# Encoder layer on one Trainium2 core: the softmax weights of the dilated attention tied to a later group of units

## The chip, the cores and the metric

The kernel runs on one core of one Trainium2 chip. Five engines work beside each other, each through its own instruction stream in order: TensorE (PE, matrix products, with its weight loads as PEld), VectorE (DVE), ScalarE (ACT), GpSimd (POOL) and SyncE (SP). SP computes nothing here; it issues nearly all DMA transfers. The metric is the device time of one execution in microseconds (us). Before the change the median of three runs is 2876.34 us (2875.6 to 2882.24).

## The reference

One layer of an encoder over 2048 tokens of 1024 features, in float32: a projection, two mixers side by side, an output projection, and a mixture of 16 experts. The part that matters here is the first mixer. For each of 8 heads it runs three banded attentions, with strides 1, 4 and 16 (the patterns 0, 1 and 2 of the kernel), and joins them by their softmax maxima and denominators:

```python
    m_all = jnp.stack(ms)
    scale = jnp.exp(m_all - jnp.max(m_all, axis=0, keepdims=True))
    numer = jnp.sum(scale[..., None] * jnp.stack(nums), axis=0)
    denom = jnp.sum(scale * jnp.stack(dens), axis=0)
    return (numer / denom[..., None]).reshape(B, S, ATTN_WIDTH)
```

## The kernel before

A float32 product is made of three PE products of rounded parts. The stages follow one another with overlap: projection and the recurrent mixer (to about 830 us), the 8 attention heads (about 860 to 1510 us), the rest of the output projection and the router, and the experts (from about 1730 us). Work that waits for nothing, projection columns (lines 236 to 238) in the first heads and the output projection (lines 858 to 860) in the last ones, is given the lowest priority and fills PE between the attention's products.

The order on each engine is made at build time by a scheduler: it simulates the program and takes, whenever an engine is free in that simulation, the ready instruction of the highest priority. On the chip the order is fixed: an instruction whose input has not come holds up everything behind it on its engine.

`att_head` computes one head. Its tokens are cut into 4 groups (g) of 512. A call of `four` does four units of 128 queries. For each group it does four units of pattern 0 and then four of pattern 1; the 16 units of pattern 2 stand between group 1 and group 2. A unit is: scores on PE (lines 645 and 646, into `pa`), bias and row maximum on DVE (line 657), exponential and row sum on ACT (line 658), transposes on PE (line 660, into `pb`), a copy of these to `eT` on DVE or ACT (lines 664 and 662), and the numerators on PE (line 690). Units of pattern 1 in groups 0 and 3 reach over the edge of the sequence: there POOL fills 64 columns of `ex` with zeros first (lines 648 and 650), and the transposes need them. POOL also lays out the queries (`qc`, lines 616 and 619).

The maxima and sums of the units stand in `st0` (pattern 0), `sg` (pattern 1) and `st2` (pattern 2). Those of patterns 0 and 2 go to DRAM (`st_d`, lines 759 and 783) and come back in another token order. Four steps for each group follow:

- `fetch`: two loads of `st_d` into `sg` (line 707), issued on SP
- `weights`: minimum, difference, exponential, sum, reciprocal and product (lines 716 to 722, on DVE, with line 718 on ACT), and a store to `cw_d` (line 723)
- `spread`: two loads that give every partition the weights, `wB` (line 728)
- `combine`: four elementwise steps on POOL (lines 733 to 736) that weigh and add the numerators of the patterns, `nt` and `n2`, and a store to `mixt_d` (line 738)

A list of due numbers says where each step stands in the program: the number 2g is the place behind pattern 0 of group g, 2g + 1 that behind its pattern 1, and numbers from 8 on are places in the next head. `after(k)` writes out what is due there. This sets priorities alone: nothing else keeps the scheduler from taking `weights` as soon as its input is there in the simulation. `n2` has one buffer for all heads, `cw` and `wB` have two.

Of the kernel before, what the change touches and what calls it, by code (L numbers as in the profile page):

```python
# [23 lines left out]
F32 = mybir.dt.float32  # L24
# [5 lines left out]
AF = mybir.ActivationFunctionType  # L30
OP = mybir.AluOpType
# [9 lines left out]
def dram_ap(t, off, ap):  # L41
    return bass.AP(tensor=t.tensor, offset=t.offset + off, ap=[list(a) for a in ap])
# [3 lines left out]
def encoder_layer(ctx, tc, x, norm1_w, w_in, q_norm_w, k_norm_w, lb_f, lb_b, o_norm_w, w_out,  # L46
                  norm2_w, w_router, w_gate, w_up, w_down, out):
    nc = tc.nc
    pe, act, dve, pool, sp = nc.tensor, nc.scalar, nc.vector, nc.gpsimd, nc.sync
# [482 lines left out]
    def att_load(p, T, h, g):  # L532

        u, s2 = h // 2, h % 2
        for j in range(2):

            x4 = p.tile([128, 4, 128], F32, name="x4", bufs=4)
            for c in range(2):
                sp.dma_start(x4[:, :, 64 * c:64 * c + 64],
                             dram_ap(qk_d, (u * S + g * 512) * 256 + 128 * j + 64 * s2,  # L540
                                     [[256, 128], [128 * 256, 4], [1, 64]]))
            T["x4", g, j] = x4
# [22 lines left out]
    def att_turn(T, g):  # L565

        qs = T["qs"].rearrange("p (r a) -> p r a", r=16)[:, :, 32 * g:32 * g + 32]
        kh, kl = (T[n][:, :, 16 + 128 * g:144 + 128 * g] for n in ("kh", "kl"))
        for j in range(2):
            pt = (pa, pb)[j]()  # L570
            for i in range(4):
                pe.transpose(pt[:, i * 128:(i + 1) * 128], T["x4", g, j][:, i], ident)
            if j == 0:

                pt = pt.rearrange("p (a r) -> p r a", r=16)
                act.activation(qs, pt, AF.Copy, scale=T["wq"])  # L576
                dve.scalar_tensor_tensor(qs[64:], pt[64:], T["wq"][64:], qs[64:].bitcast(F32),
                                         op0=OP.mult, op1=OP.subtract)
            else:
                pt = pt.rearrange("p (j r) -> p r j", r=4)  # L580
                act.activation(kh, pt, AF.Copy, scale=T["wk"])
                dve.scalar_tensor_tensor(kl, pt, T["wk"], kh.bitcast(F32), op0=OP.mult, op1=OP.subtract)

    def att_v2(T, h):
        sp.dma_start(T["vp"][2][:, :, :64], dram_ap(v_d, 64 * h, [[16 * 512, 128], [512, 16], [1, 64]]))

    def att_head(p, T, h):
# [79 lines left out]
        def four(pat, n4, st, out):  # L667


            per = 4 if pat == 2 else 2  # L670
            w, vp = 512 // per, vps[pat]
            pnum = pn([128, 512])[:, :256]
            qc = qs[:, n4 * 128:n4 * 128 + 512] if pat == 2 else qcs.pop((pat, n4 // 4))
            units = [unit(pat, n4 + i) for i in range(4)]
            eTs = [block(pat, qc[:, i * 128:], units[i:i + per], w, st[:, i:i + per], (n4 + i) % 8 >= 6)
                   for i in range(0, 4, per)]

            if pat == 0:
                todo = [[(hf, 2 * hf + u, slice(128 * u, 128 * u + 128)) for hf in range(2)] for u in range(2)]
            else:  # L680
                todo = [[(hf, u, slice(64 * u, 64 * u + 64)) for hf in range(2)] for u in range(4)]
            for pair in todo:
                for i in range(len(units[0][3])):
                    for hf, u, cols in pair:
                        e = eTs[u // per][:, u % per * w + i * 128:u % per * w + i * 128 + 128]
                        if pat == 1:
                            e = e[:, 64 * hf:64 * hf + 64]
                        elif pat == 2:
                            e = e.rearrange("p (g f a) -> p g f a", g=4, f=2)[:, :, hf, :]
                        pe.matmul(pnum[64 * hf:64 * hf + 64, cols], vp[:, units[u][3][i], :], e,  # L690
                                  start=i == 0, stop=i == len(units[0][3]) - 1)
            if pat == 0:
                act.activation(out, pnum, AF.Copy)
            elif pat == 1:
                act.activation(out.rearrange("p (j r) -> p j r", r=4), pnum.rearrange("p (r j) -> p j r", r=4), AF.Copy)
            else:
                act.activation(out, pnum.rearrange("p (r a) -> p a r", r=4), AF.Copy)
# [4 lines left out]
        late = T["late"]  # L702
# [6 lines left out]

        def weights(g):  # L710
            sg = grp[g][0]
            w = p.tile([128, 3, 4], F32, name="cw", bufs=2)
            m8 = p.tile([128, 4], F32, name="cm", bufs=2)
            d8 = p.tile([128, 4], F32, name="cd", bufs=2)
            wd = p.tile([128, 3, 4], F32, name="cdd", bufs=2)
            dve.tensor_reduce(m8, sg[:, :, :, 1].rearrange("p a t -> p t a"), axis=AX.X, op=OP.min)
            dve.tensor_tensor(w, m8[:, None, :].to_broadcast([128, 3, 4]), sg[:, :, :, 1], op=OP.subtract)
            act.activation(w, w, AF.Exp)
            dve.tensor_mul(wd, w, sg[:, :, :, 0])
            dve.tensor_reduce(d8, wd.rearrange("p a t -> p t a"), axis=AX.X, op=OP.add)  # L720
            dve.reciprocal(d8, d8)
            dve.tensor_mul(w, w, d8[:, None, :].to_broadcast([128, 3, 4]))  # L722
            sp.dma_start(dram_ap(cw_d, h * 3 * S + 512 * g, [[4, 128], [S, 3], [1, 4]]), w)
# [6 lines left out]

        def combine(g):
            sg, wB, nt = grp.pop(g)
            pool.tensor_mul(nt, nt, wB[:, :2])
            pool.tensor_mul(wB[:, 2], wB[:, 2], n2[:, 256 * g:256 * g + 256])
            pool.tensor_add(nt[:, 0], nt[:, 0], nt[:, 1])
            pool.tensor_add(nt[:, 0], nt[:, 0], wB[:, 2])
            for hf in range(2):
                sp.dma_start(mixt_d[g][64 * h:64 * h + 64, 256 * hf:256 * hf + 256],
                             nt[64 * hf:64 * hf + 64, 0])
# [1 line left out]
        grp = {}  # L741


        for g, ks in ((0, (4, 5, 6, 7)), (1, (4, 5, 6, 7)), (2, (5, 6, 7, 8)), (3, (7, 8, 9, 10))):
            for k, f in zip(ks, (fetch, weights, spread, combine)):
                late.append((8 * h + k, f is not combine, len(late), f, g))

        def after(k):
            for t in sorted(t for t in late if t[0] <= 8 * h + k):
                late.remove(t)  # L750
                t[3](t[4])

        for g in range(4):
            sg = p.tile([128, 3, 4, 2], F32, name="sg", bufs=4)
            nt = p.tile([128, 2, 256], F32, name="nt", bufs=4)
            grp[g] = sg, None, nt
            st0 = p.tile([128, 4, 2], F32, name="st0", bufs=2)
            four(0, 4 * g, st0, nt[:, 0])
            sp.dma_start(dram_ap(st_d, (h * S + 512 * g) * 2, [[2, 128], [256, 4], [1, 2]]), st0)
            after(2 * g)  # L760
            if g == 0:
                att_turn(T, 2)
                if h < 7:
                    att_load(p, T, h + 1, 0)
            elif g > 1 and h < 7:
                att_turn(T, g - 2)
                att_load(p, T, h + 1, g)
            if g < 3:
                qcs[0, g + 1] = queries(0, g + 1)
            four(1, 4 * g, sg[:, 1], nt[:, 1])  # L770
            if g < 3:
                qcs[1, g + 1] = queries(1, g + 1)
            after(2 * g + 1)
            if g == 0:
                att_turn(T, 3)
                if h < 7:
                    att_load(p, T, h + 1, 1)
            if g == 1:
                n2 = p.tile([128, S // 2], F32, name="n2", bufs=1)
                st2 = p.tile([128, 16, 2], F32, name="st2", bufs=1)  # L780
                for n4 in range(0, 16, 4):
                    four(2, n4, st2[:, n4:n4 + 4], n2.rearrange("p (a r) -> p a r", r=16)[:, :, n4:n4 + 4])
                sp.dma_start(dram_ap(st_d, (8 + h) * S * 2, [[32, 128], [1, 32]]), st2.rearrange("p r c -> p (r c)"))
                if h < 7:
                    att_v2(T, h + 1)
            if g and h < 7:
                att_values(T, h + 1, g - 1)
                if g == 3:
                    att_values(T, h + 1, 3)
        if h == 7:  # L790
            after(10)


    def op_setup(T):
# [128 lines left out]
    def heads(u):  # L923
        with mixer():
            for h in (2 * u, 2 * u + 1):
                att_head(ap_, AT, h)
# [384 lines left out]
```

## Time and profile before

| What | us |
|---|---|
| median of three runs | 2876.34 |
| the profiled execution, its own time | 2881.4 |
| its span, from the first to the last instruction | 2879.6 |
| PE busy with products, of the span | 2656.7 |
| DVE busy | 1772.3 |
| ACT busy | 1465.3 |
| POOL busy | 304.3 |

The trace is one execution; all positions below are us from the start of its span. PE is busy for 92% of the span and the other engines for 62% and less, so time can go where PE stands still. An idle stretch of another engine counts only where PE, sooner or later, waits for it. The page also gives the clock that PE was granted, as a share of full speed: it takes two levels, 1.0 (2.4 GHz) and 0.5 (1.2 GHz).

### The profile page before, as it was taken

The page shows a single profiled execution, that of the slowest core. Times are in us where ns is not written, and L with a number is a line of the kernel's source. Part 1 is how long each engine was busy: PE and PEld are TensorE (multiplying, and loading weights), DVE is VectorE, ACT ScalarE, POOL GpSimd, SP SyncE. Part 2 cuts the span into 40 slices and gives each one's busy share as a digit, 9 for nine tenths or more (in the row PEclk, how much of TensorE's full clock was granted, in tenths as well). Part 3 has the DMA queues.
Part 4 walks back from the last instruction along what each step waited for, and adds up shares of the span by engine and source line. Part 5 has one row for each costly group of instructions (what it writes and reads, how often), then busy time and mean ns, then how long its engine had stood idle before and what let it go on. Part 6 is the DMA issues. An engine that isn't in the chain of part 4 may idle for free.

```text
span 2879.6 us, 61971 instructions
## 1 busy us (share of the span) xinstructions
PE 2656.7 (92%) x24198; PEld 2447.7 (85%) x24198; DVE 1772.3 (62%) x4463; ACT 1465.3 (51%) x3056; POOL 304.3 (11%) x477
## 2 busy tenths in 40 slices
PE   8999999998998888978888959999999999999998
PEld 8899999998988777866665739999999999999997
DVE  6547787878855545665445675555555555555553
ACT  6536666667645545554333534444444444444442
POOL 0000000000011333333220010000000000000000
PEclk9999999999999989989998969999999999999999
DMA  8776877766677666767648625666666666666663
GB/s 297 241 247 204 242 217 243 215 211 207 205 229 166 148 139 153 145 139 163 146 104 269 230 86 182 209 209 206 205 205 206 206 207 207 207 208 209 209 199 105
DMA packets 613652, 563.31 MB, mean 196 GB/s; under 512 B 186208, under 2 KB 567136, under 8 KB 613360
## 3 DMA queue, kind: packets, MB, share of 16 engines
q1 hardware_dynamic: 603824, 525.72, 60.9%
q0 software_dynamic: 9536, 33.64, 5.2%
q8 instruction: 190, 3.11, 0.5%
q14 instruction: 102, 0.84, 0.1%
HBM read 466.50 MB, written 92.73 MB: 194 GB/s over the span
## 4 chain that ended last, share of the span: by engine, by line
PE 74%; DMA 14%; DVE 6%; SPq 2%; ACT 2%; issue 2%; POOL 1%; POOLq 0%; DVEq 0%; ACTq 0%
PE mpg L1227 9%; PE mpg L1229 9%; PE mpg L1228 9%; PE pm L238 6%; PE pm L237 6%; PE pm L236 6%; PE mpy L1262 4%; PE mpy L1264 4%; PE mpy L1263 4%; PE pn L690 2%; DMA st_d<-st 2%; PE pb L660 2%; PE pm L859 2%; PE pm L858 2%; DMA gz<-pf_d 2%
## 5 line engine op out<-in xcount | busy, mean ns | idle before, releaser
L1211 DVE TENSOR_TENSOR mlo<-mraw,mhi 128x1024 fp32r<-128x1024 f32 x384 | 470.1, 1224 | 465.7 <-ACT mhi L1210 465.2
L1210 ACT ACTIVATE mhi<-mraw 128x1024 fp32r<-128x1024 f32 x384 | 406.9, 1060 | 591.0 <-PE mpg L1228 404.2
L1227 PE MATMUL mpg<-xh,mhi 128*128 128x256 f32 x2048 | 579.6, 283 | 0.0
L1229 PE MATMUL mpg<-xh,mlo 128*128 128x256 f32 x2048 | 579.1, 283 | 0.0
L1228 PE MATMUL mpg<-xl,mhi 128*128 128x256 f32 x2048 | 576.5, 282 | 0.0
L1228 PEld LDWEIGHTS mpg<-xl,mhi 128*128 128x128 f32 x2048 | 387.5, 189 | 0.6
L1227 PEld LDWEIGHTS mpg<-xh,mhi 128*128 128x128 f32 x2048 | 386.6, 189 | 1.1 <-ACT xh L1183 0.4
L1229 PEld LDWEIGHTS mpg<-xh,mlo 128*128 128x128 f32 x2048 | 384.1, 188 | 0.0
L236 PE MATMUL pm<-whi,hth 128*128 128x256 f32 x1280 | 364.5, 286 | 16.3 <-ACT ast L178 10.4
L238 PE MATMUL pm<-whi,hlo 128*128 128x256 f32 x1280 | 369.0, 289 | 6.2 <-DMA hlo<-lo_d 6.2
L237 PE MATMUL pm<-wlo,hth 128*128 128x256 f32 x1280 | 365.7, 287 | 0.0
L236 PEld LDWEIGHTS pm<-whi,hth 128*128 128x128 f32 x1280 | 245.6, 192 | 18.9 <-ACT ast L178 10.9
L238 PEld LDWEIGHTS pm<-whi,hlo 128*128 128x128 f32 x1280 | 245.7, 192 | 8.9 <-DMA hlo<-lo_d 7.9
L237 PEld LDWEIGHTS pm<-wlo,hth 128*128 128x128 f32 x1280 | 244.8, 191 | 1.4 <-DVE wlo L171 0.4
L237 PE MATMUL pm<-hlo,whi 128*128 128x256 f32 x768 | 221.0, 288 | 2.6 <-DMA hlo<-lo_d 2.4
L236 PE MATMUL pm<-hth,whi 128*128 128x256 f32 x768 | 221.2, 288 | 2.1 <-ACT whi L170 1.1
L238 PE MATMUL pm<-hth,wlo 128*128 128x256 f32 x768 | 219.2, 286 | 3.8 <-DVE wlo L171 3.8
L1262 PE MATMUL mpy<-mhi,hh 128*128 128x512 f32 x512 | 205.9, 403 | 0.0
L1263 PE MATMUL mpy<-mlo,hh 128*128 128x512 f32 x512 | 203.9, 398 | 0.0
L1264 PE MATMUL mpy<-mhi,hl 128*128 128x512 f32 x512 | 202.9, 396 | 0.0
L690 PE MATMUL pn<-eT,vp 128*64 128x64 f32 (+1 forms) x2048 | 114.6, 246 | 53.8 <-DVE cw L722 13.4
L690 PEld LDWEIGHTS pn<-eT,vp 128*64 128x64 f32 x2048 | 87.4, 141 | 78.3 <-ACT qs L576 14.1
(349 smaller groups left out, 5512.2 us busy)
## 6 DMA issues: line engine op xcount, KB each, us to landing
hlo<-lo_d SPq DMA_DIRECT2D x480, 256.0 KB, 4.1
mraw<-in_w_expert_gate_dram SPq DMA_DIRECT2D x64, 1024.0 KB, 5.6
mraw<-in_w_expert_up_dram SPq DMA_DIRECT2D x64, 1024.0 KB, 5.0
mraw<-in_w_expert_down_dram SPq DMA_DIRECT2D x64, 1024.0 KB, 4.9
wraw<-in_w_in_dram SPq DMA_DIRECT2D x128, 128.0 KB, 3.9
x<-qk_d SPq DMA_DIRECT2D x128, 128.0 KB, 5.1
out_dram<-oxt SPq DMA_DIRECT2D x32, 512.0 KB, 5.9
pf_d<-est SPq DMA_DIRECT2D x96, 128.0 KB, 3.8
```

The costliest lines, as they stand in the source:

```text
L236: pe.matmul(o, l[0], r[0], start=kc == 0, stop=False)
L237: pe.matmul(o, l[0], r[1], start=False, stop=False)
L238: pe.matmul(o, l[1], r[0], start=False, stop=kc == KC - 1)
L690: pe.matmul(pnum[64 * hf:64 * hf + 64, cols], vp[:, units[u][3][i], :], e, start=i == 0, stop=i == len(units[0][3]) - 1)
L1210: act.activation(hi, src, AF.Copy)
L1211: dve.tensor_sub(lo, src, hi.bitcast(F32))
L1227: pe.matmul(o, hi[:, k, :], xh[:, k, :], start=k == 0, stop=False)
L1228: pe.matmul(o, hi[:, k, :], xl[:, k, :], start=False, stop=False)
L1229: pe.matmul(o, lo[:, k, :], xh[:, k, :], start=False, stop=k == KC - 1)
L1262: pe.matmul(o, hh[:, f, ts], hi[:, cs], start=f == 0, stop=False)
L1263: pe.matmul(o, hh[:, f, ts], lo[:, cs], start=False, stop=False)
L1264: pe.matmul(o, hl[:, f, ts], hi[:, cs], start=False, stop=f == KC - 1)
```

## The change

`after` now takes the statistics of the four units just written out. If something is due, ACT computes `one` from the last of their row sums: the sum times zero, plus one. `weights` begins with a product of its input `sg` with `one` on DVE (line 712 of the changed kernel), and `combine` with a product of two columns of `wB` with `one` on POOL (line 734). The values stay as they were, but both steps can now start only when the four units have ended. The due numbers of groups 2 and 3 are later, and with them the place behind the last head (11 in place of 10).

```diff
         def weights(g):
             sg = grp[g][0]
+            dve.tensor_scalar(sg, sg, T["one"], None, op0=OP.mult)
...
         def combine(g):
             sg, wB, nt = grp.pop(g)
+            pool.tensor_scalar(wB[:, ::2, 0:1], wB[:, ::2, 0:1], T["one"], None, op0=OP.mult)
...
-        for g, ks in ((0, (4, 5, 6, 7)), (1, (4, 5, 6, 7)), (2, (5, 6, 7, 8)), (3, (7, 8, 9, 10))):
+        for g, ks in ((0, (4, 5, 6, 7)), (1, (4, 5, 6, 7)), (2, (6, 7, 8, 9)), (3, (7, 9, 10, 11))):
             for k, f in zip(ks, (fetch, weights, spread, combine)):
                 late.append((8 * h + k, f is not combine, len(late), f, g))
 
-        def after(k):
-            for t in sorted(t for t in late if t[0] <= 8 * h + k):
+        def after(k, st=None):
+            due = sorted((t for t in late if t[0] <= 8 * h + k), key=lambda t: t[:3])
+            if due and st is not None:
+                T["one"] = p.tile([128, 1], F32, name="one", bufs=4)
+                act.activation(T["one"], st[:, 3, 0:1], AF.Copy, scale=0.0, bias=1.0)
+            for t in due:
                 late.remove(t)
                 t[3](t[4])
...
-            after(2 * g)
+            after(2 * g, st0)
...
-            after(2 * g + 1)
+            after(2 * g + 1, sg[:, 1])
...
-            after(10)
+            after(11)
```

The first place is on DVE in the second head (head 1, counted from 0). Before, the weights of its groups 0 and 1 stand right behind the four units of pattern 0 of group 2, whose statistics are `st0_14026`:

```order
L657 ISA ex_14046,st0_14026<-pa_14045,tab0_13564 128x256
L657 ISA st0_14026 128x1
L716 TENSOR_REDUCE cm_14156<-sg_13586 128x4
L716 TENSOR_REDUCE cm_14168<-sg_13758 128x4
L717 TENSOR_TENSOR cw_14155<-cm_14156,sg_13586 128x12
L717 TENSOR_TENSOR cw_14167<-cm_14168,sg_13758 128x12
```

Now the same weights stand behind the last units of pattern 1 of group 2 (`sg_14048`) and two units of pattern 0 of group 3 (`st0_14216`):

```order
L657 ISA ex_14143,sg_14048<-pa_14142,tab1_13583 128x256
L657 ISA sg_14048 128x1
L582 SCALAR_TENSOR_TENSOR kl_12697<-pb_14109,wk_12687,kh_12694 128x4x128
L657 ISA ex_14219,st0_14216<-pa_14218,tab0_13574 128x256
L657 ISA st0_14216 128x1
L657 ISA ex_14219,st0_14216<-pa_14218,tab0_13574 128x256
L657 ISA st0_14216 128x1
L712 TENSOR_SCALAR sg_13596<-sg_13596,one_14181 128x24
L712 TENSOR_SCALAR sg_13774<-sg_13774,one_14181 128x24
L717 TENSOR_REDUCE cm_14185<-sg_13596 128x4
L717 TENSOR_REDUCE cm_14198<-sg_13774 128x4
```

The weights moved back by six units, and each got a product with `one` in front.

The second place is on POOL, at the end of the same head. Before, the combining of group 0 and of group 1 (`nt_13587`, `nt_13759`) stood around the zeros for pattern 1 of group 3 (`ex_14293`), and ahead of a query of the next head (`qc_15628`) and the zeros for its first units of pattern 1 (`ex_15632`, `ex_15651`):

```order
L734 TENSOR_TENSOR wB_14237<-wB_14237,n2_13871 128x256
L650 MEMSET ex_14293 128x64 x2
L606 MEMSET tab0_16316 128x4x16
L616 COPY qc_15537<-qs_12693 128x128 x4
L607 MEMSET tab0_16316 128x4x16
L736 TENSOR_TENSOR nt_13587<-nt_13587,wB_14234 128x256
L735 TENSOR_TENSOR nt_13759<-nt_13759 128x256
L736 TENSOR_TENSOR nt_13759<-nt_13759,wB_14237 128x256
L619 COPY qc_15628<-qs_12693 128x512
L648 MEMSET ex_15632 128x64 x2
L648 MEMSET ex_15651 128x64 x2
```

Now (names are numbered anew: `nt_13597` and `nt_13775` are the two groups, `qc_15649`, `ex_15653` and `ex_15672` the next head's):

```order
L734 TENSOR_SCALAR wB_14264<-wB_14264,one_14348 128x2
L735 TENSOR_TENSOR nt_13597<-nt_13597,wB_14264 128x512
L736 TENSOR_TENSOR wB_14264<-wB_14264,n2_13895 128x256
L737 TENSOR_TENSOR nt_13597<-nt_13597 128x256
L734 TENSOR_SCALAR wB_14267<-wB_14267,one_14348 128x2
L738 TENSOR_TENSOR nt_13597<-nt_13597,wB_14264 128x256
L735 TENSOR_TENSOR nt_13775<-nt_13775,wB_14267 128x512
L736 TENSOR_TENSOR wB_14267<-wB_14267,n2_13895 128x256
L619 COPY qc_15649<-qs_12693 128x512
L648 MEMSET ex_15653 128x64 x2
L648 MEMSET ex_15672 128x64 x2
```

The zeros for group 3 now stand ahead of both combinings, and those of the next head still behind them.

## Rows read from the trace of the kernel before

**Rows 1.** Windows by stage: borders, length, busy per engine (count), clock, DMA share, GB/s
```profile
860.00:1510.00 650.00, 543.19 (x5068) 479.20 (x5067) 355.65 (x1347) 314.76 (x1084) 195.53 (x367) 0.92 0.65 145
1510.00:1600.00 90.00, 76.31 (x384) 55.48 (x384) 47.57 (x143) 35.41 (x73) 5.08 (x10) 0.89 0.79 262
1800.00:1872.00 72.00, 72.00 (x536) 67.28 (x535) 42.69 (x68) 34.20 (x48) 5.20 (x4) 1.00 0.65 209
```

**Rows 2.** Waits, 860 to 1600: who <- for whom: us in total, times, longest
```profile
POOL nt L733 <- DMA wB<-cw_d: 134.8, 18, 14.5
DVE cm L716 <- DMA sg<-st_d: 132.9, 23, 15.9
...
PE pn L690 <- DVE cw L722: 13.4, 2, 8.8
...
ACT n L697 <- POOL wB L734: 4.2, 2, 3.6
...
PE pb L660 <- POOL ex L650: 2.2, 1, 2.2
```

**Rows 3.** Timeline of DVE in head 1: start, length, instruction [idle before <- releaser]
```profile
981.89 0.08 DVE L657 DVE_READ_ACCUMULATOR2_ANT st<- 128x1 f32 x1
992.36 0.17 DVE L716 TENSOR_REDUCE cm<-sg 128x4 f32<-128x12 f32 x1 [10.39 <-DMA sg<-st_d]
...
1001.26 0.08 DVE L657 DVE_READ_ACCUMULATOR2_ANT st<- 128x1 f32 x1
...
1002.82 0.17 DVE L716 TENSOR_REDUCE cm<-sg 128x4 f32<-128x12 f32 x1 [1.47 <-DMA sg<-st_d]
...
1024.70 0.17 DVE L716 TENSOR_REDUCE cm<-sg 128x4 f32<-128x12 f32 x1 [9.40 <-DMA sg<-st_d]
```

**Rows 4.** Timeline of SP in the same place: stores of `st0` and `st2`
```profile
977.24 2.63 SPq L759 DMA_DIRECT2D st_d<-st x1
...
988.26 0.38 SPq L783 DMA_DIRECT2D st_d<-st x1
```

**Rows 5.** Timeline of PE in the same head
```profile
994.52 1.12 PE L690 MATMUL pn<-eT,vp 128*64 128x64 f32 x16 [7.26 <-DVE cd L720]
...
1036.28 0.87 PE L660 MATMUL pb<-ident,ex 128*128 128x128 f32 x6
```

**Rows 6.** Windows over 16 waits of line 716, to 3 us past each
```profile
982.00:995.40 13.40, 6.14 (x83) 5.75 (x81) 2.55 (x14) 4.30 (x15) 2.85 (x4) 0.88 0.49 131
...
1303.40:1312.80 9.40, 3.45 (x17) 2.70 (x16) 2.90 (x11) 2.43 (x10) 1.28 (x3) 0.83 1.03 213
...
1485.50:1499.30 13.80, 5.67 (x62) 4.30 (x62) 2.61 (x8) 1.46 (x4) 4.28 (x8) 0.81 0.30 88
sum 175.80, PE 84.76 PEld 72.64 DVE 40.43 ACT 40.34 POOL 45.27; mean PE 5.30 PEld 4.54 DVE 2.53 ACT 2.52 POOL 2.83
```

**Rows 7.** The window of head 1 among them, drawn out to 10 us past its wait
```profile
982.00:1002.40 20.40, 13.14 (x130) 11.68 (x129) 6.83 (x29) 8.53 (x29) 4.35 (x8) 0.83 0.51 108
```

**Rows 8.** Timeline of POOL at the end of head 1
```profile
1013.55 1.31 POOL L733 TENSOR_TENSOR nt<-nt,wB 128x512 f32<-128x512 f32 x1 [8.45 <-DMA wB<-cw_d]
...
1022.46 1.09 POOL L619 CAST qc<-qs 128x512 fp32r<-128x512 f32 x1
1023.49 0.41 POOL L648 MEMSET ex<- 128x64 f32 x4
```

**Rows 9.** Instructions by line: duration in ns, minimum/median/maximum
```profile
L112 ACT ACTIVATE osy<-oss x16: 192/203/203, 1558.5 to 1673.4; 128x1 f32<-128x1 f32 x16
```

**Rows 10.** The same view for line 717, beside which POOL works
```profile
L717 DVE TENSOR_TENSOR cw<-cm,sg x32: 159/170/1012, 916.7 to 1496.5; 128x12 f32<-128x12 f32 x32
```

**Rows 11.** The same view for a POOL copy of line 605
```profile
L605 POOL COPY tab<-tab x8: 288/306/476, 831.5 to 1315.2; 128x128 f32<-128x128 f32 x8
```

**Rows 12.** Timeline of DVE where line 717 took longest
```profile
1496.51 1.01 DVE L717 TENSOR_TENSOR cw<-cm,sg 128x12 f32<-128x12 f32 x1
```

**Rows 13.** Timeline of POOL at the same moment
```profile
1496.24 1.26 POOL L733 TENSOR_TENSOR nt<-nt,wB 128x512 f32<-128x512 f32 x1 [9.44 <-DMA sg<-st_d]
```

## The prediction

> **What bounds the kernel now.** I read the windows by stage first. In the experts' stage PE is busy for all of its 72 us at full clock, and the change touches nothing there [rows 1]. In the attention stage, from 860 to 1510, PE is busy for 543.2 of 650 us, so 106.8 us are idle, and the granted clock is 0.92: it stands at half for about 2 x 0.08 x 650 = 104 us [rows 1]. No other engine is near full there: DVE 55%, ACT 48%, POOL 30%.
>
> The waits say what PE stands behind. The largest on DVE is line 716, the first step of `weights`, for the statistics that come back from DRAM: 132.9 us in 23 waits, the longest 15.9. POOL waits 134.8 us for `wB`, and PE is found waiting directly for line 722, the end of `weights` [rows 2].
>
> The timelines of head 1 show one such wait. DVE ends the four units of pattern 0 of group 2 at 981.97 and then does nothing for 10.39 us until line 716 starts at 992.36 [rows 3]. PE, which needs a copy that is queued on DVE behind it, loses 7.26 us of these [rows 5]. SP shows why the data were late: the store of `st0` before it was issued at 977.24, that of `st2`, on which this fetch rests, only at 988.26, behind eleven us of other transfers in one queue [rows 4]. The scheduler's own simulation saw the data sooner and so put the weights too early.
>
> To size the loss I laid windows over the 16 longest waits of line 716, each to 3 us past its end: 175.8 us, of which PE is busy for 84.8 [rows 6]. So 91.0 of the stage's 106.8 idle us lie at these waits. Outside them PE is busy for 458.4 of 474.2 us, or 97%: without the waits nothing else in this trace holds PE for long.
>
> **The change, part by part.** *The weights move.* On DVE they now stand two to six units later. In head 1 that work takes from 992.53 to 1001.34, 8.8 us [rows 3], against a wait of 10.39: what is left, 1.6 us, is less than the 3.1 us that PE got through here (10.39 - 7.26) before it ran out [rows 3, 5]. I take the same for 14 of the 16 windows. Two are kept. Behind the last head no unit follows, so its window keeps its idle 13.8 - 5.7 = 8.1 us. In head 5 the order moves the weights by two units only, and its window (idle 9.4 - 3.45 = 6.0) keeps, I estimate, 2 [rows 6]. So 91 - 10 = **81 us** of PE's idle time go; bounds are 0 (data late by as much again) and 91.
>
> *The clock.* A long gap is followed by a stretch at half clock: the window of head 1 has 0.88, or 3.2 us at half, and drawn out by 7 us it has 0.83, or 6.9 us [rows 6, 7]; so 3.7 us of half clock fall on work after the gap, at a cost of 1.9. Over the stage's 104 us the cost lies between 0 (all idle) and 52 (all work); with half of it work it is 26. New, shorter gaps (below) will keep part of it, so I take **12**.
>
> *What is added.* 60 ACT steps on one column, 32 DVE steps on 24 columns, 32 POOL steps on two. Nearest rows: 0.203 us for an ACT step on one column [rows 9], 0.170 for a DVE step on 12 columns [rows 10], 0.306 for a POOL copy of 128 columns [rows 11], which I take as the upper end, with half of it as the lower. That makes 12.2 us on ACT, 5.4 on DVE and 4.9 to 9.8 on POOL. They lie beside PE, and the two busier engines have half the stage free; if that cover were gone, they would cost up to 27. The 32 new waits for `one` are short, since two units stand between its last sum and the weights. I take **2 us**, range 0 to 27.
>
> A DVE step can be longer beside POOL: line 717 has a median of 170 ns and a longest of 1012 [rows 10], and in that longest it ended at 1497.52, as POOL's line 733, running from 1496.24, ended at 1497.50 [rows 12, 13]. The Trainium skill (SBUF — State Buffer, Who interferes with whom) says that a DVE instruction with two SBUF inputs waits out a GpSimd instruction that reads SBUF, as the two share a port pair, and that a tensor_scalar in a two-port mode does so too; this speaks against the change, which adds such a step. The trace agrees for line 717, and no run here shows line 712. By that rule each of the 32 chains could be held once by 0.84 us, 27 us of DVE time in all, and the sum would be up to 27 us higher if PE had no cover.
>
> *What is late next.* This decides the size. On POOL the combining of groups 0 and 1 stands in both kernels ahead of one query and of the zeros that PE's transposes need in the next head's first units of pattern 1. In head 1 the chain from line 716 (992.36) over the store of the weights, `wB` and both combinings (line 733 starts at 1013.55) ends with these zeros at 1023.49 plus 0.41: 31.5 us [rows 3, 8]. It is made of two DRAM round trips in SP's queue, which the change does not shorten, and it now starts six units later. Between its new start (1001.34) and the transposes that need the zeros (1036.28) lie 34.9 us [rows 3, 5], but 1.5 and 9.4 of them are waits of line 716 that go too [rows 3]: 24.0 us. So POOL would be 7.5 us late, and with PE's cover of 3 it costs 4 to 5. Before, PE lost only 2.2 us to such zeros [rows 2], because the waits of DVE gave POOL time. There are 7 such places (each head but the last). Bounds are 0 and the 14.5 us of POOL's longest wait [rows 2], 101 in all; as other heads have more or less slack I take 3.5 each, nearer to the computed head: **25 us**.
>
> In the same way pattern 2 of the next head writes `n2`, whose one buffer the combining of group 3 still reads: ACT lost 4.2 us in two waits [rows 2]. That combining now stands two places later, but its data are asked for sooner after the weights. Range 0 to 3.6 (the longest) for each of 7 heads, nearest to 0 since PE has cover for 3: **2 us**.
>
> **The sum.** The profiled execution takes 2881.4 us: its span of 2879.6 and 1.8 around it. 2881.4 - 81 - 12 + 2 + 25 + 2 = 2817.4. The median of the runs lies 5.1 lower (2876.3), so I forecast 2812 us.
>
> **The rivals.** *No new gate:* SP has fewer transfers in the way of the store of the weights, POOL keeps pace, and the clock's part is larger: 2876.3 - 81 - 22 + 2 = 2775. For it: PE's 97% outside the waits. Against it: the 31.5 us of the chain in head 1.
>
> *The wait moves to POOL in full (slower):* each weights chain starts six units later, and PE runs into the missing zeros of every next head. It turns the result when PE's loss there passes 79 / 7 = 11.3 us a head, that is when POOL is about 14 us late in place of 7.5, as when the store of the weights and `wB` each stay 3 us longer in SP's queue. At POOL's longest wait, 14.5 us for each of 7 heads, it gives 2876.3 - 81 + 2 + 101 = 2898, and the clock is not regained.
>
> *SP sets the pace:* its queue is in order, and the store of `st2` came eleven us after the one before [rows 4]. If fetches slip as the units do, line 716 waits as before and the time stays at 2876. Against it: the transfers of the next head's rows, which fill that queue, do not grow with the move.
>
> *Half of it:* POOL's lateness takes 7.5 to 11.3 us a head in place of 3.5: 2812 - 25 + 53 to 79, or 2840 to 2866.
>
> **How the numbers follow.** A measurement of this kernel tells 0.3% from no change, 8.6 us: faster is below 2867.7, slower above 2885.0. Forecast (2790 to 2840): 0.50. No new gate (below 2790): 0.18. Half of it: 0.14. SP sets the pace, no change: 0.08. Slower by POOL: 0.10. So faster 0.50 + 0.18 + 0.14 = 0.82, same 0.08, slower 0.10. The range reaches from 2762, where even the two kept waits and all of the clock's 26 us are gone (2876.3 - 91 - 26 = 2759), to 2866, just under the cases of no change and slower, which with a tail of the first are the 2 in 10 left out.
>
> **What would show it.** The weights: line 716, now 717 and 712 on DVE, should have under 35 us of waits for `sg` in place of 132.9, most of it in the last head. PE's idle time in the stage should fall from 107 us to about 55, the stage's clock rise to 0.93 or 0.94. POOL's wait for `wB` should stay above 100 us, and PE (or its weight loads) should now wait for `ex` of line 648 or for the query of line 619, 3 to 5 us in most heads. The forecast is wrong if line 712 waits as long as line 716 did, if PE's gaps stay as many and as long under another name, or if the stages before 860 or after 1600 move.

## The result, and the profile after

| What | us |
|---|---|
| before, median of 4 runs | 2876.76 (2875.6 to 2882.24) |
| after, median of 4 runs | 2851.79 (2851.54 to 2855.2) |
| after / before | 0.9912, 95% interval 0.9895 to 0.9929 |
| the profiled execution of after: its time, its span | 2855.2, 2853.4 |

The change makes the kernel faster by 0.9%, 25 us. The forecast was 2812 us, a gain of 64. The direction was right and the time lies in the range, but more than half of the gain that I had worked out did not come. The rest of this document is about those 39 us.

The windows of after by stage, as in [rows 1] (length, then busy time and count of PE, PEld, DVE, ACT and POOL, granted clock, DMA share, GB/s):

```profile
860.00:1510.00 650.00, 555.97 (x5137) 490.24 (x5137) 372.13 (x1443) 330.81 (x1152) 209.46 (x409) 0.92 0.67 158
1510.00:1600.00 90.00, 85.09 (x509) 63.12 (x508) 52.12 (x126) 42.41 (x104) 0.00 (x0) 0.98 0.72 239
1800.00:1872.00 72.00, 72.00 (x536) 67.32 (x536) 42.13 (x67) 33.70 (x47) 5.18 (x4) 1.00 0.65 205
```

PE is idle for 650 - 556.0 = 94.0 us of the attention stage, against 106.8 before, and for 4.9 of the 90 behind it, against 13.7. That makes 21.6 us less; I had forecast some 54 (81 less 25 and 2). The stage's clock is still 0.92; behind it the clock rose from 0.89 to 0.98. The experts' stage is as it was.

Line 712, which now stands in front of the weights, in the view of one line (duration in ns, minimum/median/maximum; below it what ended the idle time before it):

```profile
L712 DVE TENSOR_SCALAR sg<-sg,one x32: 228/234/837, 916.4 to 1455.9; 128x24 f32<-128x24 f32 x32
...
its engine sat idle before it (us, times) until:
  ACT one L755: 4.7, 6
  DMA sg<-st_d: 2.2, 2
```

So the wait at which the change is aimed is gone: 2.2 us for `sg`, where line 716 had 132.9 [rows 2]. What stands in its place, from the waits of 860 to 1600 (who <- for whom: us in total, times, longest):

```profile
POOL wB L734 <- DMA wB<-cw_d: 169.2, 19, 20.7
...
ACT n L697 <- POOL wB L736: 42.0, 6, 12.2
...
ACT whi L170 <- DMA wraw<-in_w_in_dram: 25.0, 3, 14.6
...
ACT nt L693 <- DMA mixt_d<-nt: 24.9, 5, 9.9
...
PEld pb L660 <- POOL ex L648: 12.4, 5, 4.8
...
PE pb L660 <- POOL ex L648: 10.7, 4, 4.5
```

ACT waits 42.0 us to write the next head's `n2`, which the combining of group 3 still reads, against 4.2 before [rows 2]; 24.9 for an `nt` buffer whose sums have not been stored; 25.0 for the weights of the projection (`wraw`). Here is one such place, between head 0 and head 1, followed over five engines: the last product of the weights on DVE, then SP, POOL, ACT and PE (start, length, instruction [idle before <- releaser]). On DVE:

```profile
954.46 0.16 DVE L723 TENSOR_TENSOR cw<-cw,cd 128x12 f32<-128x12 f32 x1
```

On SP, where the store of these weights is line 724 and the loads of `wB` that follow from it are line 729:

```profile
956.66 1.87 SPq L554 DMA_DIRECT2D vp<-v_d  x4
...
963.12 4.51 SPq L539 DMA_DIRECT2D x<-qk_d  x4
967.73 1.14 SPq L724 DMA_DIRECT2D cw_d<-cw  x1
968.97 0.43 SPq L220 DMA_DIRECT2D hlo<-lo_d  x1
969.49 0.42 SPq L201 DMA_DIRECT2D v_d<-est  x1
969.96 2.39 SPq L539 DMA_DIRECT2D x<-qk_d  x4
972.45 1.50 SPq L766 DMA_DIRECT2D st_d<-st  x1
973.99 1.30 SPq L729 DMA_DIRECT2D wB<-cw_d  x2
```

On POOL, the combining of this group:

```profile
983.41 0.30 POOL L734 TENSOR_SCALAR wB<-wB,one 128x2 f32<-128x2 f32 x1 [8.48 <-DMA wB<-cw_d]
...
985.00 0.72 POOL L736 TENSOR_TENSOR wB<-wB,n 128x256 f32<-128x256 f32 x1
```

On ACT, the first write of the next `n2`:

```profile
985.76 0.38 ACT L697 ACTIVATE n<-pn 128x256 f32<-128x256 f32 x1 [12.18 <-POOL wB L736]
```

On PE, behind it:

```profile
986.20 1.12 PE L690 MATMUL pn<-eT,vp 128*64 128x64 f32 x16 [9.00 <-ACT n L697]
```

The weights are ready at 954.6. Their store leaves at 967.73, 13.1 us later, behind the next head's values, queries and keys (lines 554 and 539) in SP's one queue; PE pays 9.00 us at the end. The queue is not all of the delay: of the 31.6 us from the last product to PE's start, 13.1 pass before the store is issued, 6.3 from there to the load of `wB`, 9.4 until POOL has that load, and 2.8 on POOL and ACT. Measured in this way on the timelines, from the end of the last product to the issue of its store, the 32 stores of weights wait 150.4 us in all in the kernel before (median 2.9) and 196.7 in the changed one (median 6.2).

### The profile page after: what moved, and what is told of

The parts are those of the page before. It is cut to its first block, busy times and chain, and to the rows that moved or that the text cites. A ratio compares the mean times of both kernels' runs of the same rounds, so it can differ in the third digit from the quotient of the medians.

```text
span 2853.4 us, 62059 instructions
## 1 busy us (share of the span) xinstructions
PE 2647.6 (93%) x24198; PEld 2442.7 (86%) x24198; DVE 1776.7 (62%) x4495; ACT 1473.5 (52%) x3116; POOL 313.2 (11%) x509
## 4 chain that ended last, share of the span: by engine, by line
PE 73%; DMA 13%; DVE 7%; SPq 2%; ACT 2%; POOL 2%; issue 2%; POOLq 0%; DVEq 0%; ACTq 0%
PE mpg L1234 9%; PE mpg L1236 9%; PE mpg L1235 9%; PE pm L238 5%; PE pm L237 5%; PE pm L236 5%; PE mpy L1269 4%; PE mpy L1271 4%; PE mpy L1270 4%; DMA wB<-cw_d 2%; PE pn L690 2%; PE pb L660 2%; DMA gz<-pf_d 2%; PE pm L866 1%; PE pm L867 1%
## 5 line engine op out<-in xcount | busy, mean ns | idle before, releaser
L660 PE MATMUL pb<-ident,ex 128*128 128x128 f32 x640 | 117.1, 299 | 40.3 <-ACT ex L658 22.0
L238 PEld LDWEIGHTS pm<-hth,wlo 128*128 128x128 f32 x768 | 146.5, 191 | 5.2 <-DVE wlo L171 5.1
```

The lines of the kernel that those rows point to most:

```text
L238: pe.matmul(o, l[1], r[0], start=False, stop=kc == KC - 1)
L660: pe.transpose(pT[:, c:c + 128], ex[:, c:c + 128], ident)
```

## The experiments

The runs were made on several chips, so each is told as the ratio to the kernel before on the same chip, with the 95% interval. Every edit to the program makes the scheduler put part of the order anew; two edits that should cost little, b_non2 and a_sxp below, moved the time by 0.1%, which is inside their intervals, but how much another order alone can move it was not measured. On these chips the kernel before takes 2888 to 2901 us, against 2877 above, so a small difference between the windows or waits of two runs can also come from the chip. In the diffs, a line with - is the changed kernel (or the kernel before, for names with b_) and one with + the experiment.

### Are the new waits the price?

**a_non2** and **b_non2**: the combining reads `nt` in place of `n2` and so doesn't hold it. This leaves the numerators of pattern 2 out of the sum; the number and shapes of the instructions stay.

```diff
-            pool.tensor_mul(wB[:, 2], wB[:, 2], n2[:, 256 * g:256 * g + 256])
+            pool.tensor_mul(wB[:, 2], wB[:, 2], nt[:, 1])
```

> The changed kernel with one operand of the combining step exchanged: its third product reads the second half of `nt` instead of `n2`. Pattern 2's numerators are thereby left out of the sum; the number and shapes of instructions stay. Nothing of a head then holds `n2` past the units of pattern 2, so ScalarE no longer waits for GpSimd's combining before it writes the next head's `n2`. Theory `n2` gate: ScalarE waited 42.0 us there in six waits, and TensorE stood 9.0, 3.7, 4.9, 2.5 and 6.1 us just behind five of them, some 26 us; the time falls to about 2820 to 2828 us. Rival, the gap moves on: the transfers behind the gate (`wraw`, `nt`) are as late as before and take the place of the wait; 2843 to 2852 us, and the waits of ScalarE for DMAs grow beyond the 50 us that they have now. A time in between says how much of the gate is passed on.

> The kernel before with the same exchange: the combining step reads `nt` instead of `n2` (pattern 2's numerators are left out). There ScalarE waited for the combining only 4.2 us in two waits, so both theories give 2872 to 2878 us. It says that the exchange has no worth of its own; if this one too falls by 20 us, the gain of the exchange is not the wait that the change opened.

Measured: a_non2 0.9933 (0.9912 to 0.9954), no better than the change; b_non2 1.0012 (0.9996 to 1.0028). The wait for `n2` is gone, and others have its time. The waits of a_non2, 860 to 1600:

```profile
POOL wB L734 <- DMA wB<-cw_d: 210.8, 25, 22.4
...
ACT cw L719 <- DVE cw L718: 64.4, 15, 12.4
...
ACT nt L693 <- DMA mixt_d<-nt: 36.1, 8, 11.5
...
DVE sg L712 <- DMA sg<-st_d: 29.6, 6, 11.6
```

Line 712 waits for `sg` again, 29.6 us for 2.2, `nt` 36.1 for 24.9, and ACT's step within the weights 64.4, where the changed kernel has 19.0. PE is idle for 95.5 us of 860 to 1510, against 94.0. The trace blamed `n2` for 42 us of ACT's time, and taking that wait away gave PE nothing that can be told.

**a_z** and **a_non2_z**: VectorE writes the zeros; in the second, `n2` is left out too.

```diff
-                    pool.memset(ex[:, j * w:j * w + lo], 0.0)
+                    dve.memset(ex[:, j * w:j * w + lo], 0.0)
```

> The changed kernel with the zeros of pattern 1's score blocks written by VectorE instead of GpSimd; all else is unchanged. The prediction's term for these zeros was 25 us lost by TensorE behind GpSimd; the trace after shows TensorE waiting for them 10.7 us in four waits. Theory `n2` gate: only these 10 us can go, 2840 to 2846 us. Rival, the prediction's own sizing: 25 us go, about 2827 us. Third: VectorE gets 64 more short steps of about 0.1 us in the units that it bounds, and nothing is gained, 2850 to 2856 us.

> Both edits on the changed kernel: the combining step doesn't read `n2` (pattern 2's numerators are left out of the sum), and VectorE writes the zeros. If the two waits behind GpSimd are what the forecast mis-sized, the time comes to the forecast, 2812 us (2805 to 2822). If the lost time stands in DMAs that are late in the queue, it stays over 2835 us.

Measured: 0.9907 (0.9884 to 0.9931) and 0.9936 (0.9916 to 0.9956). The zeros, for which the prediction set down 25 us, give nothing that can be told from the change itself, and both edits together give nothing either. Neither of these two gates is the price. (a_z also gives DVE 64 short steps of 112 ns, so it doesn't price the zeros quite alone; the waits for `nt` and `wraw` were not taken away by themselves.)

### Which part of the change brings the 25 us?

**a_old**: both ties, old due numbers. **b_due**: new due numbers, no ties. **a_w**: without the tie of the sum on POOL.

```diff
# a_old
-(2, (6, 7, 8, 9)), (3, (7, 9, 10, 11))
+(2, (5, 6, 7, 8)), (3, (7, 8, 9, 10))
# b_due
-(2, (5, 6, 7, 8)), (3, (7, 8, 9, 10))
+(2, (6, 7, 8, 9)), (3, (7, 9, 10, 11))
# a_w
-            pool.tensor_scalar(wB[:, ::2, 0:1], wB[:, ::2, 0:1], T["one"], None, op0=OP.mult)
```

> Both ties on the old due numbers: groups 2 and 3 are fetched, weighed, spread and combined one unit earlier than in the changed kernel (5 to 8 and 7 to 10), each still behind its unit's `one`. Theory A, the lost time is the round trip through memory, whose stores and loads stand in one queue with the loads of the next head: what is taken from one waiter is given to another, so this order waits elsewhere and the ratio to before stays within 0.988 to 0.994, with line 712 waiting for `sg` again (over 30 us in 860 to 1600) and ScalarE's wait for `n2` under 10 us. Theory B, each wait counts by itself: the new due numbers are what freed the weights, so without them the weights wait as before and the ratio is 0.997 to 1.002.

> The kernel before with the change's due numbers alone (groups 2 and 3 one unit later), without the two ties. The ties alone on the old numbers gave 0.9901 to before. If the due numbers bring something by themselves, 0.988 to 0.995; if the scheduler puts the untied steps ahead as it did before, 0.997 to 1.003 and the weights still wait for `sg` over 80 us between 860 and 1600.

> The changed kernel without the tie of the weighted sum (the step on `wB` on GpSimd); the weights' tie and the new due numbers stay. The scheduler may then put GpSimd's combining ahead of the unit that its number names. If the tie of the weights alone brings the gain, the ratio to before is 0.988 to 0.994; if GpSimd now waits for `wB` ahead of the next unit's score copies and zeros, it is 0.996 to 1.005.

Measured: a_old 0.9901 (0.9878 to 0.9923), b_due 1.0019 (1.0002 to 1.0037), a_w 0.9927 (0.9905 to 0.9949). The ties bring it, and that of the weights is enough for most of it: what the second tie adds can't be told from nothing by these intervals. The due numbers alone bring nothing, and the wait for `sg` stays (123.2 us). What a_old waits for is another list once more: `n2` only 11.9 us, but DVE 72.3 for a `cw` buffer whose store has not left, and ACT 92.6 behind it, at the same time. My mark for a_old, over 30 us at line 712, came only in part (14.9 for the load).

### Is it SP's queue?

Added up over SP's timeline from 860 to 1600, issuing takes 458.4 us of 740 before and 459.6 after, and on top the queue itself waits in order, longest for the landing of statistics that it stored just before (the waits of SP's queue in after):

```profile
SPq L707 <- DMA st_d<-st: 40.9, 17, 3.5
```

**a_mp**: the sums (`mixt_d`) are stored by POOL. **b_mp**: the same in the kernel before. **a_sx** and **a_sxp**: 64 loads more that nothing reads, by SP and by POOL.

```diff
# a_mp, b_mp
-                sp.dma_start(mixt_d[g][64 * h:64 * h + 64, 256 * hf:256 * hf + 256],
+                pool.dma_start(mixt_d[g][64 * h:64 * h + 64, 256 * hf:256 * hf + 256],
# a_sx; in a_sxp pool for sp. In fetch, beside each of the two loads
+                sp.dma_start(p.tile([128, 8], F32, name="sx", bufs=2),
+                             dram_ap(x, (h * 4 + g) * 1024, [[8, 128], [1, 8]]))
```

> The changed kernel with the 64 stores of the sums (`mixt_d`) issued by GpSimd, which makes the sums, instead of by SyncE; they take 35.5 us of SyncE's 460 us of issuing between 860 and 1600. Theory A, the queue: the stores and fetches of the round trip leave earlier, TensorE's idle time in 860 to 1510 (94 us) falls by 15 to 30 us, ratio to before 0.981 to 0.987. Theory B, the queue's issuing is no limit: GpSimd's 35 us of issuing lie on an engine that is two thirds idle, and the ratio stays at 0.989 to 0.994.

> The changed kernel with one more small load beside each fetch of the statistics: 64 loads of 4 KB that nothing reads, from the input, so they wait for no store. They add about 64 x 0.54 = 34 us of issuing to SyncE and next to no bytes. Theory A, the queue: the time rises by 12 to 34 us, ratio to before 0.995 to 1.003. Theory B: no more than 5 us, 0.990 to 0.994.

> The 64 small loads that nothing reads, as in a_sx, but issued by GpSimd instead of SyncE. Bytes, buffers and descriptors are those of a_sx; only the queue in which they stand differs. Theory A, SyncE's queue: without the 34 us of issuing there the time goes back to that of the changed kernel, ratio to before 0.988 to 0.994. If it was the transfers themselves, or the order into which any such edit throws the schedule, it stays near that of a_sx, 0.998 to 1.003.

> The kernel before with the 64 stores of the sums issued by GpSimd; no ties, the old due numbers. Theory A: the same queue lies behind the waits of the weights, so this too gains, 6 to 20 us, ratio 0.993 to 0.998. If the weights are early by the order on VectorE alone, however soon their data come, it gains nothing: 0.998 to 1.002. If it comes to 0.985 to 0.990, the ties are worth nothing once the queue is relieved.

Measured: a_mp 0.9878 (0.9859 to 0.9896), a_sx 1.0014 (1.0000 to 1.0029), a_sxp 0.9919 (0.9899 to 0.9939), b_mp 0.9894 (0.9856 to 0.9932). The added loads in a_sx (one line's instructions, ns):

```profile
L709 SPq DMA_DIRECT2D sx<-in_x_dram x64: 328/430/1907, 902.8 to 1411.4; - x64
```

These loads, on which nothing depends, are 31.8 us of issuing by SP when added up over the timeline (64 times the median would be 27.5), and they take the whole gain of the change back: 1.0014 - 0.9919 = 0.0095 of about 2895, or some 27 us (20 to 35 by the two intervals), against the same loads issued by POOL. (POOL's went out early, from 835.6 to 1073.3, so this comparison is not of the same moments.) And b_mp is the plainest run: without any tie, with the wait at which the change is aimed nearly as long as ever, it is as fast as the changed kernel within the intervals. Its waits:

```profile
DVE cm L716 <- DMA sg<-st_d: 115.0, 21, 15.5
ACT cw L718 <- DVE cw L717: 110.5, 24, 14.9
```

The size I expected for a_mp was too large: 10 us for 35 of issuing, where I had written 15 to 30 of PE's idle time; b_mp got 30 (20 to 42 by its interval), more than the 6 to 20 I had given it.

### How far does the relief go?

All of these have the sums stored by POOL and each group's two fetches in one load. **a_mgp** and **b_mgp** have no more; **a_mgpw** has the loads of `wB` on POOL too; **a_mgpx** and **b_mgpx** those of the next head's queries and keys; **a_mgpva** has the values of pattern 0 on ACT; **a_mgpwx** both of the first two.

```diff
-            for a in (0, 1):
-                sp.dma_start(sg[:, 2 * a].rearrange("p t c -> p (t c)"),
-                             dram_ap(st_d, ((a * 8 + h) * S + 512 * g) * 2, [[8, 128], [1, 8]]))
+            sp.dma_start(sg[:, ::2].rearrange("p a t c -> p a (t c)"),
+                         dram_ap(st_d, (h * S + 512 * g) * 2, [[8, 128], [16 * S, 2], [1, 8]]))
# a_mgpw, a_mgpwx
-                sp.dma_start(wB[64 * hf:64 * hf + 64], dram_ap(cw_d, h * 3 * S + 512 * g + 256 * hf, [[0, 64], [S, 3], [1, 256]]))
+                pool.dma_start(wB[64 * hf:64 * hf + 64], dram_ap(cw_d, h * 3 * S + 512 * g + 256 * hf, [[0, 64], [S, 3], [1, 256]]))
# a_mgpx, b_mgpx, a_mgpwx
-                sp.dma_start(x4[:, :, 64 * c:64 * c + 64],
+                pool.dma_start(x4[:, :, 64 * c:64 * c + 64],
# a_mgpva
-                sp.dma_start(v0[32 * r + lo:32 * r + hi, b:b + n, :64],
+                act.dma_start(v0[32 * r + lo:32 * r + hi, b:b + n, :64],
```

> The changed kernel with the stores of the sums issued by GpSimd, and each group's two fetches of statistics put into one load (32 loads for 64). SyncE loses 35 us and about 17 us of its 460 us of issuing between 860 and 1600. Theory A, the queue: below the ratio of the stores alone (0.9878), at 0.978 to 0.986. If the queue had only been in the way of the stores of the sums, 0.986 to 0.990.

> The kernel before with both reliefs of SyncE (the sums stored by GpSimd, the two fetches of a group in one load), without ties. Theory A, the ties and the relief act on the same lost time in part: 0.985 to 0.991, above the 0.9845 of the changed kernel with the same reliefs; the difference to it is what the ties are worth with a free queue. If it comes to 0.981 to 0.985, the ties are worth nothing beside the relief.

> The changed kernel with both reliefs, and with the 64 loads of the spread weights (`wB`) issued by GpSimd too, which are 43 us of SyncE's issuing; SyncE then has about 95 us less than in the changed kernel. GpSimd's order now holds a wait for the store of the weights as well. Theory A, the queue: 0.974 to 0.982, which is where the forecast lies (0.9775). If the queue is no longer what paces the stage: 0.983 to 0.988. If GpSimd's new wait holds up the score copies and zeros behind it: over 0.988.

> The changed kernel with both reliefs, and with the 120 loads of the next head's queries and keys (line 539) issued by GpSimd; they are 73 us of SyncE's issuing. They wait for no transfer of this head, but they now stand in GpSimd's order, behind its waits for `wB` (136 us in the stage). Theory A, the queue: 0.972 to 0.982. If the loads come too late behind these waits, TensorE's transposes of lines 572 wait for them: over 0.986.

> The changed kernel with both reliefs, and with the small loads of the values of pattern 0 (line 554, 84 us of SyncE's issuing) issued by ScalarE, which is busy 377 us of the stage's 740. Theory A, the queue: 0.972 to 0.982. If ScalarE's order is the worse place (its exponentials stand behind loads that wait for the buffer `vp0`), over 0.986.

> The kernel before, without ties, with the reliefs of a_mgpx: sums stored and queries and keys loaded by GpSimd, one fetch for two. The changed kernel with these gave 0.9744 [0.9728, 0.9760]. If the ties act by themselves beside a free queue, this one stands at 0.977 to 0.984; if what they gave was only a part of what the queue took, at 0.972 to 0.977.

> The changed kernel with all of these: sums stored, spread weights and queries and keys loaded by GpSimd, one fetch for two; SyncE has some 168 us less of issuing than in the changed kernel. If each issue counts on, 0.962 to 0.970; if the stage has found its next bound, 0.972 to 0.978; if GpSimd's waits for the stores of the weights now hold up the loads behind them, over 0.980.

| Taken from SP's issuing, about | changed kernel | kernel before |
|---|---|---|
| nothing | 0.9912 (0.9895 to 0.9929) | 1 |
| sums, 35 us | 0.9878 (0.9859 to 0.9896) | 0.9894 (0.9856 to 0.9932) |
| sums, half the fetches, 52 us | 0.9845 (0.9808 to 0.9881) | 0.9863 (0.9847 to 0.9880) |
| and `wB`, 96 us | 0.9755 (0.9738 to 0.9771) | |
| or queries and keys, 125 us | 0.9744 (0.9728 to 0.9760) | 0.9841 (0.9811 to 0.9871) |
| or values of pattern 0, to ACT, 136 us | 0.9812 (0.9795 to 0.9828) | |
| `wB`, queries and keys, 168 us | 0.9740 (0.9710 to 0.9771) | |

(The sizes are those of SP's rows in the changed kernel.) With 96 us or more moved to POOL the changed kernel reaches the forecast, 2812 of 2876.8 or 0.9775, although what the kernel computes was not altered. With the issuing engine two more things change: the scheduler's order, and the DMA queue, since what POOL issues is listed in a queue of its own (q0, with 7712 packets in a_mgpx between 860 and 1510, where the kernel before has none). SP's issue time and the place in SP's DMA queue were not told apart. Past about 100 us nothing more comes. What bounds the stage there, and why ACT's queue was the worse place for the values, was not tried. Where SP's work falls by less, the steps go the right way but are small beside their intervals: a_mp stands 0.0034 below the change. The best, a_mgpx and a_mgpwx, beat both kernels: 2817 us on chips where the kernel before takes 2889 and 2890. The windows of a_mgpx, and what its waits list of the three gates:

```profile
860.00:1510.00 650.00, 577.86 (x5336) 507.83 (x5335) 401.89 (x1481) 341.18 (x1176) 332.29 (x591) 0.95 0.71 165
```

```profile
ACT nt L693 <- DMA mixt_d<-nt: 36.1, 9, 10.3
...
ACT n L697 <- POOL wB L735: 13.2, 4, 7.9
...
ACT whi L170 <- DMA wraw<-in_w_in_dram: 8.7, 4, 5.1
```

PE is idle for 72.1 us at a clock of 0.95, and the 32 stores of weights wait 114.7 us in SP's queue in all (median 2.8), against 196.7. The wait for `n2`, whose removal alone had given nothing, goes from 42.0 to 13.2 by itself. These waits of the stores do not set the time alone: measured in the same way, a_mp has 201.7 us, more than the change, and is not slower; a_mgpva has 81.8, less than a_mgpx, and is slower.

A third of the 72.1 us is now one place. Behind the last head, the output projection waits for the last sums to come back from DRAM:

```profile
1489.34 0.79 PE L864 MATMUL pm<-woh,mh 128*128 128x512 f32 x1 [22.98 <-ACT mh L856]
```

```profile
1488.65 0.63 ACT L856 ACTIVATE mh<-mx 128x512 fp32r<-128x512 f32 x1 [16.96 <-DMA mx<-mixt_d]
```

No run tried to shorten it.

**What the ties are worth beside the relief** is not settled. The rows of the table give 0.0016 and 0.0018 with intervals that overlap, and then 0.0097 with intervals that do not. In none of them is it the 0.0225 that I had forecast for the change.

## Why the prediction was wrong

*The step that failed* is "So 91.0 of the stage's 106.8 idle us lie at these waits", as the ground for taking 81 of them off. The windows show how much PE is idle beside a wait, not how much it would be idle without it [rows 6]. b_mp shows the difference: 115.0 of the 132.9 us of waiting stay, and the time falls by as much as the change's. The change takes all of the waiting away and gains 25. In the two windows PE's idle time fell by 21.6 us, where the sum had 54. What the runs show in place of the step is that a part of PE's idle time hung on the data's way through SP's queue: added issues there cost about their own time, and moving 96 us or more of them away brought the rest of the forecast gain, with 72.1 us of idle time left in a_mgpx. The order on DVE gave the waiting to others more than it took it away: ACT's wait for `n2` went from 4.2 to 42.0 us and POOL's for `wB` from 134.8 to 169.2 [rows 2]. Where the last 72 us come from is open but for the 23 behind the last head. The 97% outside the windows said that nothing else held PE then, not that nothing would.

*SP sets the pace* was among the rivals, with 8%. I let it act by one way only, the fetches, and put against it that the transfers in the queue "do not grow with the move". They need not grow: in the kernel before the issuing of this queue fills 458 of 740 us, and the row that I had read, a store 11 us after the one before it [rows 4], was a row of that. In the changed kernel the trace shows its lateness at the stores of weights and sums and at `wraw`.

*`n2`.* Set down at 2 us, since "its data are asked for sooner after the weights". ACT waited 42.0. The chain in heads 0 and 1 above shows why: asked for sooner, but the store was issued 13.1 us after the weights were ready. Yet a_non2 shows that this term, corrected, would not have mended the sum.

*The zeros.* Set down at 25 us; PE lost 10.7 in four waits (its weight loads 12.4 in five), and a_z got nothing for them. POOL was late as I had worked out (169.2 us for `wB`), but ACT was held by the same lateness earlier. The rival "Half of it" gave the right time (2840 to 2866) by this wrong way, which is luck.

*The clock.* Set down at 12 us, with 0.93 or 0.94 for the stage. It stayed at 0.92 there, with 94.0 us of gaps left of 106.8. From 1510 to 1600 it rose from 0.89 to 0.98, so some 16 us less of those 90 are at half clock (2 x 0.09 x 90); reckoned as in the prediction that is at most 8 us of the gain, an estimate. In a_mgpx the stage has 0.95.

*The added steps.* Nothing speaks against the 2 us, though no run prices them alone: the waits for `one` are 4.7 us in 6, and line 712 takes 234 ns. Its longest, 837 ns from 1024.58, ran beside POOL's lines 734 and 738 (1024.41 to 1025.38). That agrees with what the Trainium skill (SBUF — State Buffer, Who interferes with whom) says of the port pair that DVE shares with GpSimd: one instruction holds it to its end, and the other waits. But 4 of the 32 were over 400 ns, not all, and the 27 us that the rule could have cost did not come.

*What would show it wrong*: "if PE's gaps stay as many and as long under another name". They did for the most part: 94.0 us for 106.8. The two signs for the waits themselves came (2.2 us for `sg`, 169.2 for `wB`), which says that the first half of the mechanism was right; those for PE's idle time and the stage's clock did not.

## What to carry to other kernels

When many waits end at transfers of one in-order queue, price the queue first: add up its issuing in the stage, and look how long a store stands between its data and its issue. Idle time beside a wait is not the price of that wait: here 91.0 us lay beside the waits, the waits went, and 21.6 us of idle time went with them. A gate that the trace names after a change can be worth nothing (`n2`). Two cheap runs tell: put useless issues into the queue, and move useful ones out of it to an idle engine.

The Trainium skill (DMA: Bandwidth & Descriptors, Issuing engines are not separate DMA queues) says that issuing from several engines saves only the sequencer's time to initiate a transfer, which is usually small beside the transfer. Transfer by transfer the trace agrees: the loads of line 709 in a_sx take 0.43 us to issue and 2.6 to land (medians), those of `wB` in the changed kernel 0.62 and 5.5. The sum is what counted here: some 460 us of a stage of 740 in one queue, and moving 96 to 168 us of it was worth 1.6 to 1.7% of the whole kernel.

## What the runs showed that I had not expected

- A load of 4 KB that nothing waits for costs about its issue: some 27 us (20 to 35) for 64 of them in SP's queue, with 31.8 us of issuing, and next to nothing in POOL's.
- POOL's issues take longer, 0.54 us each at line 709 in a_sxp against 0.43, and are cheaper for the kernel, though POOL stands at waits for `wB` for 124.8 us in a_mgpx. The values given to ACT, with more taken from SP than by any edit but one, helped less (0.9812).
- Waits that sum to 40 us on an engine can go or come without a difference in the time that can be told (a_non2, a_old).
